# A hybrid encoder layer on one Trainium2 core: inverse rms multiplied onto the projection banks instead of onto x^T

## The chip, the cores and the metric

The kernel runs on one core of one Trainium2 chip. The core has five engines that run side by side, each with its own in-order queue of instructions: TensorE (matrix products, PE in the profile, with its weight loads as PEld), VectorE (DVE), ScalarE (ACT), GpSimd (POOL) and SyncE (SP, which here only issues DMAs). Products land in PSUM banks; everything else lies in SBUF or in device memory. The metric is device time in microseconds (us), the less the better.

## The reference

One layer over 1024 tokens of 1024 features. What matters here is its first part:

```python
def rmsnorm(x, g):
    y = xf * lax.rsqrt(jnp.mean(xf * xf, axis=-1, keepdims=True) + EPS) * g
...
    h = rmsnorm(x, g_mix_pre[l])
    proj = h @ w_in[l]
    # proj: fq, fk, fv (8 heads of 64), 8 gate columns, cq, ck, cv (8 heads of 64)
    y_fox = forgetting_attention(fq, fk, fv, f_logit)   # causal, with summed log-sigmoid gates
    y_chk = chunked_relpos_attention(cq, ck, cv, rel_bias[l])
    y = concat(rmsnorm(y_fox), rmsnorm(y_chk))
    x = x + rmsnorm(y @ w_out[l], g_mix_post[l])
    # then cross-attention into 256 memory tokens, and a squared-ReLU MLP, each with its norms
```

The inverse rms is one number for each token. The product with `w_in` sums over features, so the number can be multiplied onto a token's row of x before the product or onto its row of the product afterwards.

## The kernel before

All products are float32 made from two float32r parts: each operand is split into a high part (a rounded copy, ScalarE) and a low part (the rest, VectorE or GpSimd), and `mm3` (L174 to L176) issues three matmuls, high by high and the two mixed ones. x^T comes in two halves of 512 tokens (`th` = 0 and 1), each in 8 chunks `kc` of 128 features.

**The opening** (L1315 to L1521, an order written out by hand) loads x^T (`xf`), splits it with the gain alone (`plain_split`, L1384 and L1385) into `hT`, and computes the value banks of the first four head pairs and the gate columns in four rounds (`value_part`). In these banks tokens lie on the partitions, so the inverse rms (`rall`, from `square` and `root`) enters as one number per partition when they are emptied (`values_out`, L1438 to L1441). For queries and keys, and for the values of the later four pairs, tokens lie along the free axis. For them `spread` makes `rt[th]`, the inverse rms of 512 tokens along the free axis in all partitions; `norm` (L1413) multiplies it and the gain onto `xf`, and `norm_split` (L1418, L1419) splits the result into the same `hT` tiles again. `stock.split_now(2)` splits the first query and key weights (L311, L320), `gparts` are eleven steps of the gates (L381 to L394, log-sigmoid by exponential and logarithm, ending in `fe`), and `bias_rows` (L223 to L228) makes the relative-position rows that the chunked heads read later.

**The attention phase** is ordered by a planner, `Flow`. It keeps a clock in us (`flow.now`, 0 at its start), a cost for each step, due times for VectorE, ScalarE, GpSimd and the DMA queue (`flow.put`), and counted buffers (`Tokens`). It takes steps from several streams, the first that is ready in a fixed order: products of probabilities and values, turns (transposes of probabilities, L572 to L581), scores (L499 to L515), `side_steps`, and last `filler_steps`, which holds the projections (`project_steps`), the memory keys, the output projection and the memory values. The instructions are issued in the order that the planner finds, so each engine's queue is in that order. `flow.free` says from when an engine is free at the start.

`project_steps` computes a 128x512 bank for one pair of heads and one `th`: 24 matmuls into one of two `mm` banks. For queries and keys each half of the bank's partitions (one head) is then split: high part by ScalarE (L713, L720), low part by VectorE (L714, L721), both read from PSUM, and the bank is free when both low parts are done. Keys are copied to the other partitions by DMA. A value bank is copied by ScalarE (L693). Queries of pair 0 for `th` 0, its keys, then both for `th` 1 come first. `side_steps` starts with the transposes of the gates (`ftr`, L401) as soon as the flow clock is past 13, then copies, a running sum (`gate_scan`, L408), a store (`gate_store`), and the bias loads of the first heads wait for that store.

`u4` is a pool of 4 KB tiles (32 of them), of which `hT` holds 16 and the early values 8; the other 8 are counted tokens.

The opening's values in short: rounds (0,0), (1,0), (0,1), (1,1) of group and half; `rt0` is spread in the second round, `rt1` at the end of the third. Second phase and MLP follow with the same split products; no line of them is touched.

## Time and profile before

| what | us |
|---|---|
| median of 3 runs | 1488.63 |
| the runs | 1482.97, 1490.52, 1488.63 |
| the profiled execution | 1487.82 |
| its span, first to last instruction | 1486.0 |
| VectorE busy in the span | 921.0 |
| ScalarE busy | 804.0 |
| GpSimd busy | 387.4 |
| mean granted TensorE clock | 0.995 of full |

The profile is of one execution. Its page gives the busy time of each engine; further views give the busy time in chosen stretches, each engine's instructions in order of time, groups of equal instructions with the idle time ahead of them and what ended it, and who waited for whom. In a row such as `L714 DVE ... qs<-q,qs 64x512 fp32r<-64x512 f32 x32`, L714 is the line of the kernel, `qs<-q,qs` says what is written from what, and x32 how often. A part in square brackets such as `[7.03 <-DVE qs L714]` gives the idle time ahead of the instruction and what ended it.

### The profile page before, as it was taken

The page shows a single profiled execution, that of the slowest core. Times are in us where ns is not written, and L with a number is a line of the kernel's source. Part 1 is how long each engine was busy: PE and PEld are TensorE (multiplying, and loading weights), DVE is VectorE, ACT ScalarE, POOL GpSimd, SP SyncE. Part 2 cuts the span into 40 slices and gives each one's busy share as a digit, 9 for nine tenths or more (in the row PEclk, how much of TensorE's full clock was granted, in tenths as well). Part 3 has the DMA queues.
Part 4 walks back from the last instruction along what each step waited for, and adds up shares of the span by engine and source line. Part 5 has one row for each costly group of instructions (what it writes and reads, how often), then busy time and mean ns, then how long its engine had stood idle before and what let it go on. Part 6 is the DMA issues. An engine that isn't in the chain of part 4 may idle for free. (4 is left out here: it accounts for less than half of the span.)

```text
span 1486.0 us, 20873 instructions
## 1 busy us (share of the span) xinstructions
PE 1457.7 (98%) x7260; PEld 1228.0 (83%) x7260; DVE 921.0 (62%) x1590; ACT 804.0 (54%) x1426; POOL 387.4 (26%) x488
## 2 busy tenths in 40 slices
PE   8899999999999999999999999999999999999998
PEld 8778888888888887888888887888888888888886
DVE  4857676466466635874374687675555665656577
ACT  6637776576576753554353454555555553443442
POOL 1324565444343210431031413432223000000021
PEclk9999999999999999999999999999999999999999
DMA  8124555645437668461241446764445685445575
GB/s 327 29 87 118 127 111 106 194 135 117 116 90 186 174 189 326 143 212 58 85 170 57 138 160 230 241 237 155 150 156 170 244 344 183 142 136 205 176 249 198
DMA packets 101753, 247.90 MB, mean 167 GB/s; under 512 B 12152, under 2 KB 24576, under 8 KB 101648
## 3 DMA queue, kind: packets, MB, share of 16 engines
q1 hardware_dynamic: 97040, 238.18, 48.0%
q0 software_dynamic: 4608, 8.39, 4.1%
q8 instruction: 57, 0.93, 0.3%
q14 instruction: 48, 0.39, 0.1%
HBM read 174.64 MB, written 71.88 MB: 166 GB/s over the span
## 5 line engine op out<-in xcount | busy, mean ns | idle before, releaser
L578 DVE TENSOR_TENSOR p<-ptr,p 128x512 fp32r<-128x512 f32 (+1 forms) x152 | 92.3, 617 | 54.3 <-ACT p L581 53.6
L1916 ACT ACTIVATE whif<-ra 128x1024 fp32r<-128x1024 f32 x37 | 39.2, 1060 | 122.7 <-PE fy L175 62.6
L1918 DVE TENSOR_TENSOR wlof<-ra,whif 128x1024 fp32r<-128x1024 f32 x37 | 45.3, 1225 | 91.6 <-ACT whif L1916 91.5
L581 ACT ACTIVATE p<-ptr 128x512 fp32r<-128x512 f32 (+1 forms) x152 | 78.9, 539 | 39.9 <-PE ptr L572 39.0
L2032 POOL TENSOR_SCALAR rf<-sf 128x1 f32<-128x1 f32 x8 | 8.2, 1030 | 326.6 <-ACT jf L2017 326.3
L622 PE MATMUL pv<-p,vs 128*128 128x512 f32 (+1 forms) x304 | 85.9, 370 | 1.9 <-DVE p L578 1.9
L176 PE MATMUL fx<-vhif,wlof 128*128 128x512 f32 x168 | 65.4, 389 | 0.0
L174 PE MATMUL fx<-vhif,whif 128*128 128x512 f32 x168 | 65.4, 389 | 0.0
L175 PE MATMUL fx<-vlof,whif 128*128 128x512 f32 x168 | 65.4, 389 | 0.0
L622 PEld LDWEIGHTS pv<-p,vs 128*128 128x128 f32 x304 | 55.0, 189 | 12.5 <-DVE p L578 2.3
L1806 POOL TENSOR_TENSOR sc<-wf,wf 128x512 f32<-128x512 f32 x14 | 22.0, 1574 | 143.1 <-DMA wf<-in_w_ff 129.2
L174 PE MATMUL q<-hT_hi,whiq 128*128 128x512 f32 x128 | 52.2, 407 | 7.0 <-DVE qs L714 7.0
L174 PE MATMUL k<-hT_hi,whik 128*128 128x512 f32 x128 | 52.5, 410 | 0.0
L174 PE MATMUL mq<-h2T_hi,whimq 128*128 128x512 f32 x128 | 51.6, 403 | 0.0
L631 ACT ACTIVATE ot<-pv 128x512 f32<-128x512 f32 x64 | 38.0, 593 | 24.8 <-PE pv L622 23.2
L174 PE MATMUL yw<-whiwo,yT_hi 128*128 128x512 f32 x128 | 51.1, 399 | 0.0
L176 PE MATMUL q<-hT_hi,wloq 128*128 128x512 f32 x128 | 50.9, 398 | 0.1
L175 PE MATMUL q<-hT_lo,whiq 128*128 128x512 f32 x128 | 50.9, 397 | 0.0
L174 PE MATMUL ym<-whimo,oT_hi 128*128 128x512 f32 x128 | 50.3, 394 | 0.1
L176 PE MATMUL yw<-whiwo,yT_lo 128*128 128x512 f32 x128 | 50.4, 394 | 0.0
L175 PE MATMUL yw<-wlowo,yT_hi 128*128 128x512 f32 x128 | 50.3, 393 | 0.0
L175 PE MATMUL k<-hT_lo,whik 128*128 128x512 f32 x128 | 50.2, 392 | 0.0
(593 smaller groups left out, 4916.8 us busy)
## 6 DMA issues: line engine op xcount, KB each, us to landing
ra<-gd SPq DMA_DIRECT2D x56, 512.0 KB, 3.7
wg<-in_w_ff SPq DMA_DIRECT2D x56, 512.0 KB, 4.7
wf<-in_w_ff SPq DMA_DIRECT2D x38, 512.0 KB, 3.7
gd<-s SPq DMA_DIRECT2D x48, 256.0 KB, 2.1
od<-ot SPq DMA_DIRECT2D x64, 128.0 KB, 2.4
od<-od POOLq DMA_DIRECT2D x32, 256.0 KB, 4.5
wrawmq<-in_w_mq SPq DMA_DIRECT2D x16, 512.0 KB, 3.6
wrawmo<-in_w_mo SPq DMA_DIRECT2D x16, 512.0 KB, 3.9
```

The source lines that it names most:

```text
L174: nc.tensor.matmul(ps, lh, rh, start=start, stop=False, skip_group_check=more)
L175: nc.tensor.matmul(ps, lh, rl, start=False, stop=False, skip_group_check=more)
L176: nc.tensor.matmul(ps, ll, rh, start=False, stop=stop, skip_group_check=more)
L578: flow.put("V", at, 0.56 if dead else 0.7, lambda: nc.vector.tensor_sub(pl[:, live, :], tr[:, live, :], f(ph[:, live, :])), done)
L581: flow.put("S", flow.end, 0.49 if dead else 0.6, lambda ph=ph, tr=tr, live=live: nc.scalar.activation(ph[:, live, :], tr[:, live, :], AF.C ...
L622: nc.tensor.matmul(pv[:, :, q0 * P:(q0 + k1 - k0) * P], v, x[:, :, k0:k1, :].rearrange("p m k q -> p m (k q)"), start=c == 0 and m == 0, s ...
L631: nc.scalar.activation(box["t"][:, :, :, ::step], pv.rearrange("p m (k q) -> p m k q", q=P), AF.Copy)
L1806: eng.tensor_sub(sc[:, k1], r0[:, k0], r1[:, k0])
L1916: nc.scalar.activation(ah, ra, AF.Copy)
L1918: nc.vector.tensor_sub(al, ra, f(ah))
L2032: nc.gpsimd.tensor_scalar(r, ssf[b][:, 0:1], ssf[b][:, 1:2], EPS, op0=ALU.add, op1=ALU.add)
```

## The change

The second scaling and split of x^T in the opening goes. `hT` keeps the split of x^T with the gain alone. Each query, key or later value bank is multiplied by `rt[th]` as it is emptied: by one VectorE operation into a new float32 tile (`qn`, two buffers) for queries and keys, which are then split from that tile, or straight into `vt` for values. `rt` gets a tag of its own with two buffers. The counted `u4` tokens go from 8 to 7, the `u4` pool from 32 to 31 tiles, and the descriptor scratch of GpSimd's DMAs from 4096 to 1024 bytes per partition. In the opening the first two weight splits move ahead of the third round's `values_out`, the gate steps are no longer interleaved with norms, and squares 6 and 7 move ahead of the second round's `values_out`. The bias rows and their store become planned steps due at flow time 8, the gate transposes may start at flow time 5 instead of 13, and VectorE counts as free from 3.0 instead of 5.0.

```diff
-        return up.tile(list(shape), dt, tag="u4", bufs=32, name=name)
+        return up.tile(list(shape), dt, tag="u4", bufs=31, name=name)
...
-            dict(... ot=3, u4=8,
+            dict(... ot=3, qn=2, u4=7,
...
                 yield (0.681, lambda: kc or there((what, n)) and free["mm"].ready() and
-                       (th or free["u4"].ready(u) and (what != "k" or free["klo"].ready(2))))
+                       (what == "v" or free["qn"].ready()) and (th or free["u4"].ready(u) and (what != "k" or free["klo"].ready(2))))
...
-                flow.put("S", flow.end, 0.6, lambda th=th, ps=ps, cs=cs: nc.scalar.activation(vt[n][:, cs], ps, AF.Copy),
+                flow.put("V", flow.end, 0.7, lambda th=th, ps=ps, cs=cs: nc.vector.tensor_tensor(vt[n][:, cs], ps, rt[th], op=ALU.mult),
...
+            def scaled(ps=ps, box=box, th=th, nm=f"{what}n{n}_{th}"):
+                box["x"] = p1.tile([P, HT], F32, tag="qn", bufs=2, name=nm)
+                nc.vector.tensor_tensor(box["x"], ps, rt[th], op=ALU.mult)
+
+            def halves(at, box=box, th=th, cs=cs):
+                free["mm"].give(at)
+                left = all_of(("qn", what, n, th), 2, free["qn"].give)
+                for a, (own, oth) in enumerate(HALVES):
...
+                            nc.scalar.activation(kd[n, a][own, cs], box["x"][own], AF.Copy)
...
+                            nc.vector.tensor_sub(kl[n, a][own, cs], box["x"][own], f(kd[n, a][own, cs]))
...
+            flow.put("V", flow.end, 0.7, scaled, halves, 1)
...
-        yield 0.87, lambda: flow.now > 13.0 and free["tr"].ready(2)
+        yield 0.87, lambda: flow.now > 5.0 and free["tr"].ready(2)
...
-            r = p1.tile([P, HT], F32, tag="ot", bufs=3, name=f"rt{th}")
+            r = p1.tile([P, HT], F32, tag="rt", bufs=2, name=f"rt{th}")
...
-        def norm(th, kc):
-            x = xf[th][kc // 2][:, kc % 2, :]
-            nc.vector.scalar_tensor_tensor(x, x, gp[:, kc:kc + 1], rt[th], op0=ALU.mult, op1=ALU.mult)
-
-        def norm_split(th, kc):
-            x = xf[th][kc // 2][:, kc % 2, :]
-            h, l = hT[th].hi(kc), hT[th].lo(kc)
-            nc.scalar.activation(h, x, AF.Copy)
-            nc.vector.tensor_sub(l, x, f(h))
...
         gparts, gate_turn, gate_scan, gate_store = forget_gates()
+        stock.split_now(2)
         values_out(0, 1, V)
-        for call in gparts[:4]:
+        for call in gparts:
             call()
-        stock.split_now(2)
...
         values_out(1, 1, W)
         bias_rows(0)
-        bias_rows(1)
-        flow.put("D", 14.0, 0.55, lambda: nc.sync.dma_start(rd, rows[0]))
-        flow.free.update(V=5.0, S=3.0)
+        flow.put("V", 8.0, 2.0, lambda: bias_rows(1), lambda at: flow.load(at, lambda: nc.sync.dma_start(rd, rows[0])), 3)
+        flow.free.update(V=3.0, S=3.0)
...
-    nc = bacc.Bacc("TRN2", target_bir_lowering=False, num_devices=1, dynamic_dma_scratch_size=4096)
+    nc = bacc.Bacc("TRN2", target_bir_lowering=False, num_devices=1, dynamic_dma_scratch_size=1024)
```

More of the change, by code (lines that the diff above doesn't have):

```diff
@@ new lines, in project_steps, with hi, lo, then @@
+            free["qn"].take()
+            box = {}
+            def scaled(ps=ps, box=box, th=th, nm=f"{what}n{n}_{th}"):
[5 more added lines that the diff above has]
+                for a, (own, oth) in enumerate(HALVES):
+                    def hi(a=a, own=own):
+                        if what == "q":
+                            pv = box["x"].rearrange("p (a b) -> p a b", b=P)[:, :, ::1 if kind == "f" else -1]
+                            dst = qs[n, a].rearrange("p (a b) -> p a b", b=P)[:, th * 4:th * 4 + 4, :]
+                            nc.scalar.activation(dst[own], pv[own], AF.Copy, scale=-0.125)
+                        else:
+                            nc.scalar.activation(kd[n, a][own, cs], box["x"][own], AF.Copy)
+                    def lo(a=a, own=own, oth=oth):
+                        if what == "q":
+                            pv = box["x"].rearrange("p (a b) -> p a b", b=P)[:, :, ::1 if kind == "f" else -1]
+                            dst = qs[n, a].rearrange("p (a b) -> p a b", b=P)[:, th * 4:th * 4 + 4, :]
+                            nc.vector.scalar_tensor_tensor(dst[oth], pv[own], -0.125, f(dst[own]), op0=ALU.mult, op1=ALU.subtract)
+                        else:
+                            nc.vector.tensor_sub(kl[n, a][own, cs], box["x"][own], f(kd[n, a][own, cs]))
+                    copy = lambda x, own=own, oth=oth: nc.sync.dma_start(f(x[oth, cs]), f(x[own, cs]))
+                    def then(at, a=a, lo=lo, copy=copy):
+                        if what == "k":
+                            flow.load(at, lambda: copy(kd[n, a]), part, 2.3)
+                        flow.put("V", at, 0.63, lo, lambda end: (left(end), part(end) if what == "q" else flow.load(
+                            end, lambda: copy(kl[n, a]), part, 2.3)), 1)
+                    flow.put("S", at, 0.6, hi, then, 1)
@@ L1490, in build @@
         spread(1, d, "pv")
-        for kc in range(6, KC):
-            norm(0, kc)
-        for kc in range(KC):
-            norm_split(0, kc)
         W = value_banks(1, 1)
```

50 lines of the change are left out of this document (2 added, 48 removed).

## The prediction

> **What bounds the kernel now.** First the page: busy time by engine, and the 40 slices of 37.15 us.
>
> ```profile
> span 1486.0 us, 20873 instructions
> PE 1457.7 (98%) x7260; PEld 1228.0 (83%) x7260; DVE 921.0 (62%) x1590; ACT 804.0 (54%) x1426; POOL 387.4 (26%) x488
> PE   8899999999999999999999999999999999999998
> ```
>
> TensorE is busy for all but 28.3 us of the span, and only the first, second and last slices show gaps. The change removes no matmul, so it can pay only where TensorE stands still or runs slowly. The busy time in stretches of 10 us around the opening's end, and three later ones of 100 us, show where (columns after the length: busy us and instructions of PE, PEld, DVE, ACT, POOL, then the granted clock, DMA share, GB/s):
>
> ```profile
> 60.00:70.00 10.00, 9.23 (x41) 7.32 (x39) 9.07 (x14) 6.29 (x12) 3.54 (x3) 1.00 0.37 105
> 70.00:80.00 10.00, 3.74 (x9) 2.97 (x10) 7.44 (x14) 5.00 (x9) 5.18 (x4) 0.73 0.31 96
> 80.00:90.00 10.00, 10.00 (x47) 7.87 (x45) 3.65 (x3) 2.30 (x4) 0.00 (x0) 0.93 0.46 136
> 200.00:300.00 100.00, 99.15 (x533) 83.70 (x532) 60.61 (x168) 66.74 (x139) 50.13 (x82) 1.00 0.58 143
> 300.00:400.00 100.00, 100.00 (x552) 85.59 (x551) 62.77 (x187) 68.87 (x148) 41.05 (x57) 1.00 0.46 117
> 400.00:500.00 100.00, 98.06 (x620) 87.91 (x619) 62.34 (x181) 68.69 (x142) 41.59 (x53) 1.00 0.55 139
> ```
>
> From 70 to 80 us TensorE does 3.74 us of work at a granted clock of 0.73 while VectorE is full before it (9.07 of 10 us). From 200 to 500 us TensorE loses 2.8 us in all. The list of waits names the releaser of the gap; beside it the longest later wait on VectorE:
>
> ```profile
> PE q L174 <- DVE qs L714: 7.0, 1, 7.0
> PE pv L622 <- DVE p L578: 1.9, 1, 1.9
> ```
>
> The timeline of each engine says what was late (start, duration, engine, line, what). TensorE:
>
> ```profile
> 63.40 0.39 PE L176 MATMUL q<-hT_hi,wloq 128*128 128x512 f32 x1
> 63.63 0.39 PE L174 MATMUL k<-hT_hi,whik 128*128 128x512 f32 x1
> 68.84 0.39 PE L176 MATMUL k<-hT_hi,wlok 128*128 128x512 f32 x1
> 76.26 0.77 PE L174 MATMUL q<-hT_hi,whiq 128*128 128x512 f32 x1 [7.03 <-DVE qs L714]
> 80.24 1.58 PE L401 MATMUL ftr<-ident,fe 128*8 128x128 f32 x8
> 81.58 0.48 PE L174 MATMUL q<-hT_hi,whiq 128*128 128x512 f32 x1
> ```
>
> ScalarE and VectorE over the same time:
>
> ```profile
> 65.16 4.26 ACT L1418 ACTIVATE hT_hi<-xf 128x512 fp32r<-128x512 f32 x8
> ...
> 70.75 1.06 ACT L311 ACTIVATE whiq<-wrawq 128x1024 fp32r<-128x1024 f32 x1
> 72.65 1.19 ACT L713 ACTIVATE qs<-q 64x512 fp32r<-64x512 f32 x2
> 67.53 0.23 DVE L394 SCALAR_TENSOR_TENSOR fe<-fz,fe 128x64 f32<-128x64 f32 x1
> 67.67 3.70 DVE L1419 TENSOR_TENSOR hT_lo<-xf,hT_hi 128x512 fp32r<-128x512 f32 x6
> 71.28 1.66 DVE L1441 SCALAR_TENSOR_TENSOR vs<-v,rall,vs 128x256 fp32r<-128x256 f32 x4
> 73.34 1.37 DVE L228 COPY rrow<-rrow 8x511 f32<-8x511 f32 x1
> 74.73 1.39 DVE L714 SCALAR_TENSOR_TENSOR qs<-q,qs 64x512 fp32r<-64x512 f32 x2
> ```
>
> The first query bank is complete at 63.8 us (63.40 + 0.39), the first key bank at 69.2. Both `mm` banks are then full, and the next query product needs one back. Emptying the query bank is queued behind the second split of the right half of x^T (L1418, L1419), the value banks and the bias rows: ScalarE reaches it at 72.65, VectorE at 74.73, and TensorE resumes at 76.26. By then its second-half operands are also only just there (the last L1419 ends at 71.4).
>
> **The change part by part.** *The stall.* The key product's 24 matmuls start every 0.2265 us ((68.84 − 63.63)/23), so without a wait the next one would start at 69.07. It and what follows up to 81.58 are nine q matmuls and eight gate transposes: 12.51 us. At full pace the nine take 2.04. The eight transposes take 1.34 slow (81.58 − 80.24); matmul pace there is 0.44 ((80.24 − 76.26)/9), about half speed, so I take 0.67. Sum 2.71, **gain 9.8 us**: 7.2 of standing and 2.6 of slow clock. Without the second part being true it is 7.2.
>
> [...] The trace shows 5.3 us of slow work here, so the rows decide.
>
> *What has to be early for this.* Removed from the opening (groups between 36 and 77 us):
>
> ```profile
> L1413 DVE SCALAR_TENSOR_TENSOR xf<-xf,gp,rt 128x512 f32<-128x512 f32 x16 | 14.2, 938 | 0.0
> L1419 DVE TENSOR_TENSOR hT_lo<-xf,hT_hi 128x512 fp32r<-128x512 f32 x16 | 9.9, 687 | 3.4 <-ACT hT_hi L1418 3.4
> L1418 ACT ACTIVATE hT_hi<-xf 128x512 fp32r<-128x512 f32 x16 | 8.5, 617 | 0.0
> ```
>
> That is 24.1 us of VectorE and 8.5 of ScalarE, all ahead of the first bank. Two rows of ScalarE, the spread of `rt1` and its last gate column, place what is left:
>
> ```profile
> 46.47 0.60 ACT L1408 ACTIVATE rt<-rt 128x512 f32<-128x512 f32 x1 [5.67 <-PE rt L1406]
> 53.01 0.31 ACT L1440 ACTIVATE fcol<-v,rall 128x8 f32<-128x8 f32 x1
> ```
>
> ScalarE goes from `rt1` (over at 47.1) straight to the two first weight splits (2 x 1.06), the value banks and the gates. The last value banks are full when the first query product starts (63.40 − 23 x 0.2265 = 58.2) and take about 2 us (four times 0.4 on each engine, L1441 for one of them), so VectorE is free by 60.5. The scaling of the first query bank starts when that bank is full, near 63.8, and frees it after one VectorE instruction, near 64.6: 4.5 us before TensorE asks. The bias rows (1.4 us and a little) now follow behind it; even ahead of it with the gates' scan they would free the bank by 69. Their store and reload serve only the chunked heads, which come after all four pairs of the others.
>
> *The gate transposes* move from flow time 13 to 5, about 63 us. They stand in TensorE's in-order queue, and everything behind them waits if `fe` is late. Its chain waited in before for ScalarE and for VectorE's norms; alone it is the eight sums of `fz`, two table loads like the one below, and ten small operations like L394 (0.23):
>
> ```profile
> 54.01 0.70 DVE L381 TENSOR_TENSOR fz<-fcol,bfgt 128x8 f32<-128x8 f32 x8
> 63.70 1.28 ACT L391 ACT_TABLE_LOAD   x1 [4.74 <-DVE fe L390]
> 82.48 2.28 DVE L408 TENSOR_TENSOR_SCAN fla<-fea 8x1024 f32<-8x1024 f32 x1 [4.92 <-ACT fea L405]
> ```
>
> That is 0.7 + 2.6 + 2.3, some 5.6 us, from the last gate column, which ScalarE writes near 51.4 (47.1 + 2.1 + the 2.2 that the column took behind the last split) instead of 53.3: ready at 57 to 58.5, 5 us ahead. Cost 0. Their scan (2.3 us on VectorE) ends near 68, so the store of its row and the first bias loads, which now stand ahead of the key copies on SP, hold back no copy: the first key half is split near 71.
>
> *Added work.* Forty bank scalings (16 query, 16 key, 8 value banks), each a 128x512 VectorE operation with one PSUM and one SBUF input; that is the form of L578. Eight ScalarE copies of value banks go. The split halves then read SBUF, not PSUM:
>
> ```profile
> L578 DVE TENSOR_TENSOR p<-ptr,p 128x512 fp32r<-128x512 f32 x72 | 49.3, 688 | 23.2 <-ACT p L581 22.8
> L693 ACT ACTIVATE vt<-v x8: 578/598/606, 267.2 to 441.4; 128x512 f32<-128x512 f32 x8
> L721 DVE TENSOR_TENSOR kl<-k,kd x32: 664/690/696, 76.1 to 461.9; 64x512 fp32r<-64x512 f32 x32
> L1413 DVE SCALAR_TENSOR_TENSOR xf<-xf,gp,rt x16: 739/747/1792, 36.2 to 64.2; 128x512 f32<-128x512 f32 x16
> L320 POOL TENSOR_TENSOR wloq<-wrawq,whiq x16: 1274/1295/1927, 56.5 to 392.4; 128x512 fp32r<-128x512 f32 x16
> ```
>
> 40 x 0.688 = 27.5 us on VectorE, spread over some 410 us: its share there rises from 62% to 68 or 69%. ScalarE loses 4.8 us; its split halves go from 0.59 to about 0.62 (L1418, from SBUF), 64 x 0.025 = 1.6 back. Neither is the bound.
>
> The 64 low halves become operations with two SBUF inputs. With a PSUM input those of the keys never varied (0.664 to 0.696); L1413, with two SBUF inputs, went from 0.747 to 1.792 beside GpSimd's weight split, which itself went from 1.295 to 1.927. So a collision costs up to 1.05 us of VectorE and 0.63 of GpSimd. GpSimd is busy 41 to 50%; with that share colliding, for half the price each, VectorE pays 64 x 0.45 x 0.52 = 15 us, another 3.6%.
>
> [...]
>
> What lands on TensorE I bound by −1 us (a bank held for 0.7 instead of some 2.6 us; of the 2.8 us lost between 200 and 500 us no listed wait is for such a bank) and by +34 us (one full collision price for half of the 64). TensorE's waits on VectorE with VectorE at 62% are the 1.9 above and some smaller; at 72% they may grow by half. I take **+1.0**.
>
> *The rest at 0.* `u4` with 31 buffers: no wait named here is for one; if the memory keys start late for it, scores and turns run meanwhile, and without these TensorE would stand for as long as the delay. The smaller descriptor scratch touches the accumulating DMAs of GpSimd:
>
> ```profile
> od<-od POOLq DMA_DIRECT2D x32, 256.0 KB, 4.5
> ```
>
> There are 32 in some 380 us, so hardly ever more than a few in flight; if each had to wait for the last to land, GpSimd would lose 4.5 us a time, 144 in all, and the turns with it. The two weight splits, moved ahead, find GpSimd idle and free their raw buffers, so the next weight load on SP only gets earlier. The key copies come 0.7 us later for their bank; the next pair's products cover that, as they cover the whole way to the first scores now, and uncovered it would delay the first scores by 0.7.
>
> Sum: 1487.82 − 9.8 + 1.0 = **1479.0** for the profiled execution; the runs' median stands 0.8 above it (1488.63), so 1479.8.
>
> **The rivals.** *Most of it is given back in attention*: VectorE at 72% with collisions makes score and turn waits of 3 to 9 us. For: ScalarE and VectorE already pass work to each other in 23.2 us of idle ahead of L578; against: 38% of VectorE is free. Time 1483 to 1487, say 1485.
>
> *The gates come late.* `fe` was ready at 67.76 in before; if it were that late again, TensorE would stand from 63.2 for 4.5 us and then run slowly for as much as 2.6: gain 9.8 − 7.1, about 1486. Against: the chain's 5.6 us.
>
> *Slower: collisions in the low halves.* It decides from nine or ten of the 64 that each put a full 1.05 us on TensorE's path; with 20 it is 21 us: 1488.6 − 9.8 + 21 = 1500; with half of them, 1513. For: GpSimd also normalises the probabilities that the turns wait for. Against: query and key evacuations lie 5.4 us apart, and no score waits on the pair at hand.
>
> **How the numbers follow.** Forecast 0.66 (1476 to 1481.5); given back 0.18; gates late 0.06; slower 0.10. About 0.5%, 7.4 us, is what a measurement can tell here (the three runs spread over 7.5 us), so faster means below 1481.2. The forecast nearly all (0.62) and a little of the case given back (0.03): 0.65; within: 0.25; slower 0.10. The range: the full 9.8, the −1 and 3 us of scatter give 1474.5; upwards it takes in the cases up to 1487.
>
> **What would show it.** Right: no wait of TensorE between 58 and 90 us; granted clock 1.00 from 70 to 90; the gate transposes near 63 us, unslowed; the scaling right behind each bank; about 27 us more VectorE between 70 and 480 us, with some low halves above 1 us; first scores some 10 us earlier. Wrong: a gap at 63 us ahead of the transposes, a new wait on `qn` or on VectorE among the scores and turns, or an attention stage that ends less than 8 us earlier than before.

## The result and the profile after

The changed kernel takes 1475.31 us (median of 5 runs, 1474.34 to 1475.99) beside 1484.23 us of the kernel before in the same comparison (5 runs, 1482.53 to 1490.52): ratio 0.9929, 95% interval 0.9904 to 0.9955. Run twice more beside other kernels it gave 0.9914 (0.9899 to 0.9929) and 0.9921 (0.9902 to 0.9940). The middle one of the three is 0.79% faster, some 11.7 us of 1486; the forecast was 8.8 us. The profiled executions differ by 12.5 us (1486.0 and 1473.5). The median of three runs from which the prediction started, 1488.63, lay at the high end: in five later comparisons, 17 runs each, the kernel before has medians of 1485.08 to 1487.80.

The page of the changed kernel: span, busy time, slices.

```profile
span 1473.5 us, 20806 instructions
PE 1453.8 (99%) x7260; PEld 1225.4 (83%) x7260; DVE 931.9 (63%) x1598; ACT 793.7 (54%) x1402; POOL 398.2 (27%) x488
PE   8999999999999999999999999999999999999998
```

The gap of the second slice is gone. Idle TensorE time fell from 28.3 to 19.7 us, and its busy time from 1457.7 to 1453.8 with the same 7260 matmuls: some of them had run slowly. The same stretches as in the prediction (length; busy us and instructions of PE, PEld, DVE, ACT, POOL; granted clock, DMA share, GB/s):

```profile
60.00:70.00 10.00, 10.00 (x49) 8.13 (x49) 5.34 (x9) 3.81 (x6) 5.04 (x4) 1.00 0.33 107
70.00:80.00 10.00, 10.00 (x46) 8.26 (x45) 4.34 (x7) 2.52 (x4) 0.00 (x0) 1.00 0.31 72
80.00:90.00 10.00, 10.00 (x46) 8.28 (x45) 4.33 (x8) 2.52 (x4) 0.89 (x2) 1.00 0.51 143
200.00:300.00 100.00, 99.41 (x530) 83.51 (x528) 69.06 (x179) 65.94 (x137) 52.06 (x76) 1.00 0.56 138
300.00:400.00 100.00, 100.00 (x542) 85.57 (x542) 68.57 (x177) 63.08 (x132) 41.98 (x55) 1.00 0.48 120
400.00:500.00 100.00, 98.94 (x635) 88.94 (x634) 71.35 (x199) 71.46 (x149) 40.33 (x51) 1.00 0.58 155
```

From 70 to 80 us TensorE is full at a clock of 1.00 (before: 3.74 us at 0.73). VectorE's share from 200 to 500 us went from 62% to 70%, and TensorE lost 1.65 us there instead of 2.79.

VectorE's timeline of the changed kernel around the first query bank (start, duration, engine, line, what; in brackets the idle time before it and its releaser); below it the row of the gate transposes, with the shortest, median and longest ns and the first and last start:

```profile
58.68 0.23 DVE L394 SCALAR_TENSOR_TENSOR fe<-fz,fe 128x64 f32<-128x64 f32 x1
58.83 1.65 DVE L1442 SCALAR_TENSOR_TENSOR vs<-v,rall,vs 128x256 fp32r<-128x256 f32 x4
64.10 0.69 DVE L708 TENSOR_TENSOR qn<-q,rt 128x512 f32<-128x512 f32 x1 [3.62 <-PE q L176]
67.22 2.28 DVE L408 TENSOR_TENSOR_SCAN fla<-fea 8x1024 f32<-8x1024 f32 x1 [0.25 <-ACT fea L405]
...
70.45 0.69 DVE L708 TENSOR_TENSOR kn<-k,rt 128x512 f32<-128x512 f32 x1 [0.23 <-PE k L176]
```

```profile
L401 PE MATMUL ftr<-ident,fe x8: 270/272/273, 63.9 to 64.7; 128*8 128x128 f32 x8
```

VectorE is done with the value banks at 60.5 and waits 3.6 us for TensorE; the bank is scaled 0.2 us after it is full and free at 64.8. `fe` is ready at 58.9, 5.0 us ahead of the transposes, which run at 0.27 us each.

The groups of VectorE from 60 to 500 us (busy, mean ns of one | idle before them); the first two of before, the others of the changed kernel:

```profile
L714 DVE SCALAR_TENSOR_TENSOR qs<-q,qs 64x512 fp32r<-64x512 f32 x32 | 22.0, 689 | 23.3 <-ACT qs L713 18.6 <-PE q L176 4.1
L721 DVE TENSOR_TENSOR kl<-k,kd 64x512 fp32r<-64x512 f32 x32 | 22.0, 688 | 25.1 <-ACT kd L720 24.6
```

```profile
L726 DVE SCALAR_TENSOR_TENSOR qs<-qn,qs 64x512 fp32r<-64x512 f32 x32 | 27.3, 853 | 5.8 <-ACT qs L718 4.9
L728 DVE TENSOR_TENSOR kl<-kn,kd 64x512 fp32r<-64x512 f32 x32 | 27.3, 852 | 9.4 <-ACT kd L720 8.9
L708 DVE TENSOR_TENSOR kn<-k,rt 128x512 f32<-128x512 f32 x16 | 11.0, 688 | 11.3 <-PE k L176 11.3
L708 DVE TENSOR_TENSOR qn<-q,rt 128x512 f32<-128x512 f32 x16 | 11.0, 686 | 12.1 <-PE q L176 12.0
L693 DVE TENSOR_TENSOR vt<-v,rt 128x512 f32<-128x512 f32 x8 | 5.5, 682 | 1.4 <-PE v L176 1.4
```

The forty scalings take 27.5 us. The 64 low halves, now with two SBUF inputs, went from 44.0 to 54.6 us.

Three rows divide the span: the first query product, the first score and the first product of the memory queries (first and last start behind the durations). Before, then after:

```profile
L174 PE MATMUL q<-hT_hi,whiq x128: 387/389/767, 57.8 to 416.6; 128*128 128x512 f32 x128
L499 PE MATMUL sf0g<-kd,qs x12: 277/389/497, 97.3 to 112.2; 128*128 128x512 f32 x5, 128*128 128x256 f32 x4, 128*128 128x384 f32 x3
L174 PE MATMUL mq<-h2T_hi,whimq x128: 389/389/486, 627.5 to 811.7; 128*128 128x512 f32 x128
```

```profile
L174 PE MATMUL q<-hT_hi,whiq x128: 387/389/486, 58.4 to 406.7; 128*128 128x512 f32 x128
L499 PE MATMUL sf0g<-kd,qs x12: 277/363/475, 87.9 to 103.7; 128*128 128x512 f32 x5, 128*128 128x256 f32 x4, 128*128 128x384 f32 x3
L174 PE MATMUL mq<-h2T_hi,whimq x128: 389/389/486, 614.9 to 799.1; 128*128 128x512 f32 x128
```

First query product to first score, A: 39.5 to 29.5 us. First score to first memory query, B: 530.2 to 527.0. From there to the end: 858.5 and 858.6. The first query product itself starts anywhere between 55.8 and 59.1 us whatever the kernel, so A and B tell apart what spans blur. They come from the one profiled execution of each kernel, as differences of starts given to 0.1 us, and the ratio comes from all its runs. The profiled executions of remove_only and values_on_act were the slowest of theirs (1479.46 beside a median of 1475.13, 1485.89 beside 1481.75), so their B is on the high side. All profiled kernels:

```
kernel             ratio  (95% interval)       A      B      A+B
before             -                           39.5   530.2  569.7
before_again       0.9998 (0.9985 to 1.0012)   39.7   526.9  566.6
scratch_only       1.0003 (0.9992 to 1.0015)   39.3   529.4  568.7
u4_only            1.0041 (1.0026 to 1.0057)   43.6   529.7  573.3
buffers_only       1.0047 (1.0033 to 1.0060)   40.9   532.5  573.4
bias_late          0.9988 (0.9975 to 1.0000)   37.7   527.9  565.6
short_gap          0.9952 (0.9933 to 0.9970)   34.5   529.3  563.8
remove_only        0.9927 (0.9913 to 0.9941)   29.5   531.9  561.4
remove_again       0.9932 (0.9913 to 0.9951)   29.5   530.1  559.6
values_only        0.9937 (0.9917 to 0.9956)   29.5   525.5  555.0
after              0.9929 (0.9904 to 0.9955)   29.5   527.0  556.5
after_again        0.9914 (0.9899 to 0.9929)   29.5   525.9  555.4
after_third        0.9921 (0.9902 to 0.9940)   29.4   526.1  555.5
placement_back     0.9914 (0.9898 to 0.9930)   29.5   526.1  555.6
scale_twice        0.9918 (0.9899 to 0.9937)   30.1   527.4  557.5
low_from_bank      0.9928 (0.9915 to 0.9942)   31.2   527.1  558.3
values_on_act      0.9974 (0.9962 to 0.9987)   29.5   537.2  566.7
order_kept         0.9930 (0.9912 to 0.9948)   29.5   526.3  555.8
order_moved        0.9987 (0.9977 to 0.9998)   29.5   536.1  565.6
```

### The profile page after: what moved, and what is told of

It is laid out like the page before. It is cut to its first block, busy times and chain, and to the rows that moved or that the text cites. A ratio compares the mean times of both kernels' runs of the same rounds, so it can differ in the third digit from the quotient of the medians.

```text
span 1473.5 us, 20806 instructions
## 1 busy us (share of the span) xinstructions
PE 1453.8 (99%) x7260; PEld 1225.4 (83%) x7260; DVE 931.9 (63%) x1598; ACT 793.7 (54%) x1402; POOL 398.2 (27%) x488
## 5 line engine op out<-in xcount | busy, mean ns | idle before, releaser
L176 PE MATMUL k<-hT_hi,wlok 128*128 128x512 f32 x128 | 50.2, 392 | 0.0
L175 PE MATMUL mq<-h2T_lo,whimq 128*128 128x512 f32 x128 | 50.0, 391 | 0.0
```

What stands on the lines that cost most here:

```text
L175: nc.tensor.matmul(ps, lh, rl, start=False, stop=False, skip_group_check=more)
L176: nc.tensor.matmul(ps, ll, rh, start=False, stop=stop, skip_group_check=more)
```

## The experiments

### The parts of the change in the opening

**before_again**: the kernel before, unchanged.

> The kernel before, unchanged, for a second profile. Theory A (the time beyond the forecast comes from a stall late in attention that hangs on one DMA and on the clock): the wait of 7.0 us near 69 us is there again to within 0.2 us, and the stall near 512 us (1.9 us, then a granted clock below 1 for some 4 us) differs from the first profile by a microsecond or more, so the span differs by 1 to 4 us. Rival B (the change's edits in attention gave it): the second profile repeats the first, stall near 512 us included, and the span is 1486 within 1 us.

The wait of 7.0 us repeats, and A is 39.7. The wait of 1.9 us at `pv`, the longest of attention in the first profile, shrinks to 0.2, and the slow matmuls behind it are gone too; B is 3.3 us shorter. Theory A holds: the profile from which the prediction started had this much more in attention than the next one of the same kernel.

**remove_only**: the normalisation of x^T alone is taken out, with nothing in its place, so queries, keys and the later values leave out the inverse rms.

```diff
-        for kc in range(2):
-            norm(0, kc)
...
-        for kc in range(2, KC):
-            norm_split(1, kc)
```

> The kernel before without the second scaling and split of x^T, and without anything in its place: queries, keys and the later values leave out the inverse rms. All other edits of the change are absent. Theory A (the gain is the opening's stall alone, the added bank scalings cost TensorE nothing): the wait near 69 us is gone, the first score starts 9 to 10 us earlier than in the kernel before, and the time equals the changed kernel's to within 2 us (1473 to 1477). Rival B (the added scalings or collisions cost TensorE something that the gain hides): it is 3 us or more faster than the changed kernel. Rival C (the change's other edits, placement or buffers, give part of the gain): it is 3 us or more slower than the changed kernel.

A = 29.5, the same as with the whole change: the removal alone earns the opening's 10 us. The time, 1475.13 us beside 1485.59, is that of theory A.

**placement_back**: the changed kernel with the gates, the bias rows and VectorE's booked start as before.

```diff
-        yield 0.87, lambda: flow.now > 5.0 and free["tr"].ready(2)
+        yield 0.87, lambda: flow.now > 13.0 and free["tr"].ready(2)
...
-        flow.put("V", 8.0, 2.0, lambda: bias_rows(1), lambda at: flow.load(at, lambda: nc.sync.dma_start(rd, rows[0])), 3)
-        flow.free.update(V=3.0, S=3.0)
+        bias_rows(1)
+        flow.put("D", 14.0, 0.55, lambda: nc.sync.dma_start(rd, rows[0]))
+        flow.free.update(V=5.0, S=3.0)
```

> The changed kernel with three placements of the kernel before: gate transposes from flow time 13, bias rows ahead of the planned steps with their store at 14, VectorE free from 5.0. Theory A (the removed work alone clears the way for the first bank): no wait near 69 us, time within 1.5 us of the changed kernel, first score up to 4 us later but TensorE filled with the next projections. Rival C (the placement does part of it): a wait of 1 us or more comes back between 64 and 80 us, 2 us or more slower than the changed kernel.

0.9914 and A = 29.5: these three moves neither cost nor earn anything that can be told.

### Which queue was late

**bias_late**: the kernel before, with the second bias rows behind the bank instead of ahead of it.

```diff
-        bias_rows(1)
-        flow.put("D", 14.0, 0.55, lambda: nc.sync.dma_start(rd, rows[0]))
+        flow.put("V", 19.0, 2.0, lambda: bias_rows(1), lambda at: flow.load(at, lambda: nc.sync.dma_start(rd, rows[0])), 3)
```

> The kernel before with the bias rows planned at flow time 19 instead of ahead of the first low halves, nothing else. Theory A (the first bank is held by what stands ahead of it on VectorE): the wait of 7.0 us shrinks by the rows' 1.9 us to 5.1, the nine query products behind it still run at half speed for about 4 us, time 2 us less than the kernel before. Rival H (ScalarE's order, not VectorE's, holds the bank): the wait shrinks by less than 1 us.

The wait only falls from 7.0 to 6.15 us, which is the sign of rival H and not the 5.1 of theory A. Timeline of TensorE, ScalarE and VectorE in this kernel:

```profile
76.71 0.76 PE L174 MATMUL q<-hT_hi,whiq 128*128 128x512 f32 x1 [6.15 <-DVE qs L714]
73.95 1.19 ACT L713 ACTIVATE qs<-q 64x512 fp32r<-64x512 f32 x2
75.17 1.39 DVE L714 SCALAR_TENSOR_TENSOR qs<-q,qs 64x512 fp32r<-64x512 f32 x2 [0.94 <-ACT qs L713]
```

VectorE is now early and waits 0.94 us for ScalarE, which runs its own queue without a pause (splits, value banks, two weight splits) until 73.95. The two queues were nearly equally late: taking the rows' 1.9 us (72.85 to 74.71 in the kernel before) out of one gains 0.9 and moves the bound to the other.

**short_gap**: the same, and without six of the eight splits of the second half.

```diff
-        for kc in range(2, KC):
-            norm_split(1, kc)
```

> As bias_late, and six of the eight second splits of the right half of x^T left out (chunks 2 to 7 of it keep the split with the gain alone, so queries and keys of the right half mix scaled and unscaled chunks). Theory A: VectorE and ScalarE reach the first bank some 3.5 us earlier still, the wait is 1.5 to 3 us. If the slow pace needs a gap longer than that, the products behind it run at full pace and the time is 8 to 9 us below the kernel before; if any gap of some us brings it, 5.5 to 7 us below.

TensorE's timeline:

```profile
73.19 0.77 PE L174 MATMUL q<-hT_hi,whiq 128*128 128x512 f32 x1 [3.05 <-DVE qs L714]
73.76 0.63 PE L175 MATMUL q<-hT_lo,whiq 128*128 128x512 f32 x1
...
75.46 0.63 PE L176 MATMUL q<-hT_hi,wloq 128*128 128x512 f32 x1
...
76.18 0.40 PE L175 MATMUL q<-hT_lo,whiq 128*128 128x512 f32 x1
```

A gap of 3.05 us is followed by six matmuls some 0.43 us apart instead of 0.2265; the seventh (75.89) is on pace again, 2.7 us after the first. A falls by 5.0 us (39.5 to 34.5), 3.95 by the shorter gap and about 1 by the shorter slow stretch. The gap of 3.05 us lies at the end of the expected 1.5 to 3, and the pace behind it is slow all the same. The time falls by 0.48%, some 7 us, the upper end of the case with the slow pace.

### The buffers

**buffers_only, u4_only, scratch_only**: the kernel before with 31 `u4` buffers (tokens 7) and the smaller descriptor scratch, and with each alone.

```diff
-        return up.tile(list(shape), dt, tag="u4", bufs=32, name=name)
+        return up.tile(list(shape), dt, tag="u4", bufs=31, name=name)
...
-            dict(s=2, tr=2, pv=2, mm=2, sp=5, p=2, klo=4, bias=2, raw=2, w=2, ot=3, u4=8,
+            dict(s=2, tr=2, pv=2, mm=2, sp=5, p=2, klo=4, bias=2, raw=2, w=2, ot=3, u4=7,
...
-    nc = bacc.Bacc("TRN2", target_bir_lowering=False, num_devices=1, dynamic_dma_scratch_size=4096)
+    nc = bacc.Bacc("TRN2", target_bir_lowering=False, num_devices=1, dynamic_dma_scratch_size=1024)
```

> The kernel before with 31 u4 tiles, 7 counted tokens and the descriptor scratch of 1024 bytes, nothing else. Theory A: no change that can be told, within 3 us of the kernel before; the accumulating DMAs of GpSimd issue in 0.84 us and land in 4.5 us as before. Rival C (buffers reorder the end of attention for the better): 3 us or more faster. Rival D (they cost something): slower by 2 us or more, with waits of GpSimd between the accumulating DMAs above 24.6 us in all.

> The kernel before with 31 u4 tiles and 7 counted tokens, scratch as it was. Theory F (the 7 us of the three buffer edits together come from the planner, which finds another order with one token less): 1.003 to 1.006 of the kernel before, first memory key product some 5 us later after the first score than in the kernel before. Rival G (they come from the descriptor scratch): within 0.1% of the kernel before.

> The kernel before with 1024 bytes of descriptor scratch instead of 4096 and nothing else. Theory F: within 0.1% of the kernel before, accumulating DMAs issue in 0.84 and land in 4.5 us. Rival G: 1.003 to 1.006, with longer issues or landings of these DMAs.

The scratch costs nothing (1.0003). One `u4` buffer less costs the kernel before 0.41%, some 6 us, and with the scratch 0.47%. Theory F of u4_only has the size right and the place wrong: the first memory key product comes 1.9 us later after the first score, not 5, and A grows by 4.1. In buffers_only GpSimd's waits between its accumulating DMAs stay at 23.9 us, so the time of theory D came without its sign. ScalarE and TensorE in `u4_only`:

```profile
85.31 0.59 ACT L720 ACTIVATE kd<-k 64x512 fp32r<-64x512 f32 x1 [10.87 <-PE q L175]
87.49 0.47 PE L174 MATMUL k<-hT_hi,whik 128*128 128x512 f32 x1 [2.05 <-DVE kl L721]
```

ScalarE needs the second `kd` tile and waits 10.87 us for the last query product: the four weight tiles of the first query and key live in `u4` and no token counts them. With 16 tiles of x^T, 8 of the value banks, these 4, two `qs` and two `kd`, 32 are wanted. Behind the late split the key bank stays full, and TensorE waits. The changed kernel has the same wait, 3.92 us long:

```profile
75.72 0.63 ACT L720 ACTIVATE kd<-kn 64x512 fp32r<-64x512 f32 x1 [3.92 <-PE q L175]
```

There the bank went free with the scaling, 4.6 us earlier (L708 on `kn`: 70.45 + 0.69), and TensorE does not wait. low_from_bank, next, takes this early return away, and a wait of TensorE comes back.

**low_from_bank**: the changed kernel, with the low halves read from the bank, which is given back after both; the low halves then leave out the inverse rms.

```diff
-                free["mm"].give(at)
-                left = all_of(("qn", what, n, th), 2, free["qn"].give)
...
+                held = all_of(("mmq", what, n, th), 2, free["mm"].give)
+                back = all_of(("qn", what, n, th), 2, free["qn"].give)
+                left = lambda end: (held(end), back(end))
...
-                            nc.vector.tensor_sub(kl[n, a][own, cs], box["x"][own], f(kd[n, a][own, cs]))
+                            nc.vector.tensor_sub(kl[n, a][own, cs], ps[own], f(kd[n, a][own, cs]))
```

> The changed kernel, but the low halves of queries and keys read the bank in PSUM and not the scaled tile, so a bank is held until both low halves are done, and the low halves have one SBUF input each; what they compute leaves out the inverse rms, the high halves keep it. Theory A (the collisions cost VectorE some 10 us and TensorE nothing): the low halves go back to 0.69 us each, the sum of VectorE between 60 and 500 us falls by about 10 us, the time stays within 2 us of the changed kernel. Rival B (collisions cost TensorE something): 2 us or more faster. Rival E (a bank that is free after one operation is what makes the changed kernel proof against fewer buffers, which cost the kernel before 7 us): 3 us or more slower, with a wait of a projection on a low half.

The groups of VectorE, and TensorE's timeline after the gap:

```profile
L727 DVE SCALAR_TENSOR_TENSOR qs<-q,qs 64x512 fp32r<-64x512 f32 x32 | 22.0, 688 | 5.9 <-ACT qs L719 5.0
L729 DVE TENSOR_TENSOR kl<-k,kd 64x512 fp32r<-64x512 f32 x32 | 22.0, 687 | 9.6 <-ACT kd L721 9.1
```

```profile
75.15 0.50 PE L174 MATMUL k<-hT_hi,whik 128*128 128x512 f32 x1 [1.28 <-DVE kl L729]
75.48 0.39 PE L175 MATMUL k<-hT_lo,whik 128*128 128x512 f32 x1
```

The low halves are back at 44.0 us, so their 10.6 us are the price of the second SBUF input. Two rows of the changed kernel show how it falls (shortest, median and longest ns):

```profile
L726 DVE SCALAR_TENSOR_TENSOR qs<-qn,qs x32: 684/687/2981, 65.5 to 422.6; 64x512 fp32r<-64x512 f32 x32
L728 DVE TENSOR_TENSOR kl<-kn,kd x32: 665/690/1673, 71.8 to 452.8; 64x512 fp32r<-64x512 f32 x32
```

The median is as before. The 24 of the 64 that no GpSimd instruction overlaps take at most 0.69 us; of the 40 others, twelve take more than 1 us, the longest 2.98. Yet without the collisions nothing gets faster: 1474.89 us beside 1472.57 of the changed kernel on the same chip, intervals overlapping. This run does not show that they cost TensorE nothing, because it adds waits of its own: A is 1.7 us longer by the wait that the early return had hidden, and attention has a wait of 2.64 us at a score (459.30, `sc6g`) that the changed kernel lacks. Without the latter B would be some 2 us shorter than the changed kernel's mean of 526.3 (527.1 − 2.64 = 524.5), so up to about 2 us of collisions on TensorE's path stay possible, by one profile.

### The load on VectorE

**scale_twice**: the changed kernel, every scaling issued twice, those of the value banks too, and the planner told 1.4 us for both.

```diff
-                nc.vector.tensor_tensor(box["x"], ps, rt[th], op=ALU.mult)
+                for _ in range(2):
+                    nc.vector.tensor_tensor(box["x"], ps, rt[th], op=ALU.mult)
...
-            flow.put("V", flow.end, 0.7, scaled, halves, 1)
+            flow.put("V", flow.end, 1.4, scaled, halves, 1)
```

> The changed kernel with each of the 40 bank scalings issued twice, the planner told 1.4 us for both: 27.5 us more on VectorE, which is then at about 78% between 100 and 480 us. Theory A (VectorE has slack enough, the scalings cost TensorE nothing): within 3 us of the changed kernel. Rival B (VectorE is near the point where it decides): 6 us or more slower, with waits of TensorE on L578 or the scores' reductions above 5 us in all.

The scalings take 55.0 us instead of 27.5 and the ratio is 0.9918, beside 0.9921 of the changed kernel (**after_third**) on the same chip. In its profile A is 0.7 us and B 1.1 us longer than in the changed kernel, and the time can't be told apart. VectorE has that much room; most of attention's length does not hang on it.

> The changed kernel, unchanged, beside the others on one chip. Theory A: 0.9915 to 0.9940 of the kernel before, its span within 2 us of the first profile; TensorE's waits between the first score and the memory queries again 2 to 4 us in all.

> The changed kernel, unchanged, for a third profile and for times beside the others. Theory A: 10.0 us from the first query product to the first score less than in the kernel before (29.5 against 39.5), and 0.991 to 0.994 of its time.

Both repeat the first comparison: 0.9914 and 0.9921, A = 29.5 and 29.4, and in after_again 3.12 us of waits of TensorE between the first score and the memory queries. The span of after_again is 2.8 us shorter than that of the first profile (1470.7 beside 1473.5), somewhat more than the 2 us allowed.

### Why attention became shorter

B was 528.8 us in the mean over the first three kernels of the table and is 526.3 in the three profiles of the changed kernel. Five kernels ask where this comes from.

**remove_again, values_only, values_on_act**: the first has neither scalings nor the value move, the second moves the value copies alone to VectorE, the third is the changed kernel with them back on ScalarE. All three leave out the inverse rms of the later values, the first two that of queries and keys as well. The edit of the second, beside that of remove_only:

```diff
-                flow.put("S", flow.end, 0.6, lambda th=th, ps=ps, cs=cs: nc.scalar.activation(vt[n][:, cs], ps, AF.Copy),
+                flow.put("V", flow.end, 0.7, lambda th=th, ps=ps, cs=cs: nc.vector.tensor_copy(vt[n][:, cs], ps),
```

> The kernel before without its normalisation of x^T, a second time (this leaves out the factor 1/rms of query, key and value). The length of the stretch from the first score to the first product of the memory queries is what is asked for: 526.9 to 530.2 us in three profiles with the order of the kernel before, 531.9 in the first of this kernel, 525.9 to 527.0 in three of the changed kernel. If the 2.5 us are scatter of one run to the next: between 526 and 530 here. If the new emptying of the banks earns them: 529 or more again, and a time of 0.992 to 0.994 of the kernel before.

> The same kernel, with the eight value banks copied by VectorE and not by ScalarE (the factor 1/rms is still left out); query and key banks are emptied as in the kernel before. If relieving ScalarE's queue of these copies is what shortens attention: a stretch of 526 to 527.5 us, and a time of 0.991 to 0.992. If the early return of query and key banks does it: 529 to 532 us and the ratio of the kernel with the normalisation removed, 0.9927. If it is scatter: no order between this one and that.

> The changed kernel, with the eight value banks copied by ScalarE as before (this leaves out the factor 1/rms of the values); query and key banks are scaled by VectorE as in the change. If the early return of query and key banks shortens attention: 526 to 527.5 us, 0.991 to 0.992. If the value copies do it: 529 to 532 us, 0.9927 to 0.994. If it is scatter: anything from 526 to 532, and a time that can't be told from the changed kernel's 0.992.

With the copies on VectorE B is 525.5, with them on ScalarE 530.1 and 531.9 (nothing else changed) or 537.2 (in the changed kernel, more than any of its three cases allowed). In time the first pair can't be told apart (0.9937 and 0.9932; values_only lacks the 0.991 to 0.992 of its first case), the second clearly: 0.9974 against 0.9914 to 0.9929. The 8 copies are only 4.8 us of ScalarE, so either that load or the order that the planner writes out must be what counts.

**order_kept, order_moved**: the changed kernel, with the engine and the booking taken apart. The first copies on ScalarE but is booked on VectorE; the second scales on VectorE, as in the change, but is booked on ScalarE.

```diff
 order_kept
-                flow.put("V", flow.end, 0.7, lambda th=th, ps=ps, cs=cs: nc.vector.tensor_tensor(vt[n][:, cs], ps, rt[th], op=ALU.mult),
+                flow.put("V", flow.end, 0.7, lambda th=th, ps=ps, cs=cs: nc.scalar.activation(vt[n][:, cs], ps, AF.Copy),
 order_moved
-                flow.put("V", flow.end, 0.7, lambda th=th, ps=ps, cs=cs: nc.vector.tensor_tensor(vt[n][:, cs], ps, rt[th], op=ALU.mult),
+                flow.put("S", flow.end, 0.6, lambda th=th, ps=ps, cs=cs: nc.vector.tensor_tensor(vt[n][:, cs], ps, rt[th], op=ALU.mult),
```

> The changed kernel; the eight value banks are copied by ScalarE (this leaves out the factor 1/rms of the values), but the planner books the copy on VectorE as in the change, so the order of all other work stays that of the changed kernel. With planner and copy both on ScalarE the ratio was 0.9974, the stretch from the first query product to the first product of the memory queries 566.7 us, against 555.4 to 556.5 in three profiles of the changed kernel. If the order that the planner writes out makes the difference: 0.991 to 0.993 and 555 to 558 us. If ScalarE's load by eight copies does it (4.8 us of it): 0.996 to 0.998 and 563 us or more.

> The changed kernel whole, with the planner booking the scaling of the eight value banks on ScalarE though VectorE does it. If the order that the planner writes out makes the difference: 0.996 to 0.998, 563 us or more from the first query product to the first memory query. If ScalarE's load does it: 0.991 to 0.993 and 555 to 558 us.

This separates them: order_kept 0.9930 and B = 526.3, order_moved 0.9987 and B = 536.1, on the same chip. Together with the changed kernel (both on VectorE, 0.9914 to 0.9929) and values_on_act (both on ScalarE, 0.9974) all four pairs of engine and booking are measured: booking decides, not the engine. What the other order does is seen at the hand-over from attention to the output. SyncE's issues in order_moved, then in the changed kernel (start, time of the issues, x count):

```profile
547.74 2.71 SPq L1053 DMA_DIRECT2D yw<-yd  x4
550.50 0.43 SPq L214 DMA_DIRECT2D g_mix_post<-in_g_mix_post  x1
552.16 0.33 SPq L214 DMA_DIRECT2D g_mem_pre<-in_g_mem_pre  x1
552.53 1.20 SPq L1004 DMA_DIRECT2D xtw<-in_x  x2
554.74 1.62 SPq L298 DMA_DIRECT2D wrawmv<-in_w_mv  x2
```

```profile
544.38 2.46 SPq L1053 DMA_DIRECT2D yw<-yd  x4
546.94 0.42 SPq L298 DMA_DIRECT2D wrawmv<-in_w_mv  x1
548.09 0.33 SPq L214 DMA_DIRECT2D g_mix_post<-in_g_mix_post  x1
```

The changed kernel issues one of the last two loads of the memory value weights ahead of the gains and of `xtw`; in order_moved both stand behind them. ScalarE and TensorE of order_moved show what follows; then the window of 560 to 580 us of order_moved, and TensorE's wait and the same window of the changed kernel:

```profile
565.09 1.06 ACT L311 ACTIVATE whimv<-wrawmv 128x1024 fp32r<-128x1024 f32 x1 [6.50 <-DMA wrawmv<-in_w_mv]
566.20 0.80 PE L174 MATMUL mv<-whimv,mT_hi 128*128 128x512 f32 x1 [2.81 <-ACT whimv L311]
```

```profile
560.00:580.00 20.00, 15.85 (x55) 11.82 (x55) 7.80 (x8) 7.09 (x8) 0.00 (x0) 0.83 0.70 240
```

```profile
563.69 0.50 PE L174 MATMUL mv<-whimv,mT_hi 128*128 128x512 f32 x1 [0.49 <-ACT whimv L311]
```

```profile
560.00:580.00 20.00, 18.75 (x81) 14.69 (x80) 11.70 (x14) 8.32 (x13) 0.00 (x0) 1.00 0.82 283
```

TensorE stands for 2.81 us and then runs at half pace (0.43 us a matmul until 572.7). In the changed kernel the same product waits 0.49 us and the clock of that window is 1.00. This place holds 5.7 of the 9.1 us by which B of order_moved exceeds the changed kernel's first profile (first `mv` at 546.8, mq at 623.6: 76.8; changed: 543.8 and 614.9: 71.1); the other 3.4 lie ahead of it, a wait of 2.05 us for a memory key weight among them.

## Why the prediction was right and wrong

Part by part, in the two profiled executions on which the sum was built: A fell by 10.0 us (forecast 9.8), B fell by 3.2 (forecast: 1.0 longer), the first query product came 0.6 later and the rest took 0.1 more. Together that is 12.5 us less where 8.8 were forecast. The measured 1475.31 us lies below the 1476 to 1481.5 that the prediction gave its forecast. The step that failed is the term for attention, and a starting time that was too high hid behind it.

**Right: the opening.** A fell by 10.0, 10.2 and 9.9 us in three pairs of profiles (before and after, before_again and after_again, scratch_only and after_third); the forecast was 9.8. Of before's 28.3 us of idle TensorE, 7.0 stood here, and the slow stretch behind it is gone. That this gap was paid twice, by standing and by the slow stretch, is borne out from the other side by short_gap (A 5.0 us shorter: 3.95 and about 1). That the slow part came out so close is partly luck: it repeated in the three profiles above, but behind an equal gap of 7.03 us in buffers_only the slow matmuls lasted 2.7 us instead of 5.3, which would make the gain some 1.3 us less.

**Right: what had to be early.** `fe` was ready at 58.9 (57 to 58.5 forecast), the transposes ran at 63.9 at full speed, and the scaling stood right behind its bank, so "the gates come late" fell. VectorE was named as the late queue with ScalarE 2 us ahead of it; bias_late shows that ScalarE was nearly as much the bound. The change empties both, so the sum did not suffer.

**Right in mechanism, off in size: collisions.** 10.6 us of VectorE against 15. That is 0.17 us a piece in the mean (10.6 / 64), against the 0.23 assumed (0.45 x 0.52). Some low halves above 1 us were named as a sign, and twelve are. In before, with one PSUM input, 34 of the 64 overlap a GpSimd instruction and none takes more than 0.70 us; in the changed kernel, with two SBUF inputs, 40 do, and the twelve are among them. VectorE's busy time between 70 and 480 us rose by 32.7 us (254.8 to 287.5) and not by the 27 named, which left the collisions out. The slower rival needed nine or ten collisions that reach TensorE in full; low_from_bank leaves room for about 2 us of them.

**Wrong: "I take +1.0" for attention.** The step was that TensorE's waits grow by half when VectorE is fuller, and that nothing works the other way. They shrank. From the first score to the first memory query TensorE stood for 6.05, 4.63 and 7.00 us in before, before_again and scratch_only, and for 4.11, 3.12 and 3.31 in the three profiles of the changed kernel. The means, 5.9 and 3.5, make 2.4 of the 2.5 us by which B shrank; TensorE's busy time there stayed at 523. Against the +1.0 this is 3.5 us, about the 3 us by which the gain was larger than forecast (11.7 against 8.8). The load itself may have been sized rightly: in scale_twice 27.5 us more of it go with 5.31 us of waiting and a B 1.1 us longer, by one profile, and the times can't tell it. Waits of 3 to 9 us, as "given back in attention" has them, are out by the same run.

What went is a wait for a weight of the memory keys (0.9, 0.7 and 1.8 us before) and two short ones of the value turns (0.5 and 0.3); waits of 0.5 and 0.2 at `pv` are new. The prediction left out that the planner writes the order of every queue from the engine and cost booked for each piece, so that a changed booking re-sorts loads that come some 100 us later as well. The memory key wait bears this out: it stands in all eleven profiled kernels that book the value banks on ScalarE, 0.2 to 2.8 us long, and in none of the eight that book them on VectorE, whichever engine works. In time the booking of these eight pieces is worth 0.57% between order_moved and order_kept, and 0.58 to 0.73% between order_moved and the changed kernel, which use the same engine; that is several times the term. But the bad order of order_moved is not the order of the kernel before, so this does not say how much of before's 2.5 us is booking and how much scatter (526.9 to 530.2): values_only has B at 525.5 and yet no shorter time than remove_again. That share stays open.

**Wrong: "`u4` with 31 buffers at 0".** The edit is not free: 6 us in the kernel before, with a wait of 10.87 us on ScalarE. The sum did not show it because the early return of the bank hides it in the changed kernel; low_from_bank, without that return, has A 1.7 us longer. The prediction asked only about memory keys and missed the four weight tiles that no token counts.

**The starting point.** The time predicted was 4.5 us above the measured one. By the first comparison alone (1484.23 − 1475.31 = 8.9 us) the gain equals the forecast and all of the 4.5 is the high median of the first three runs; by the middle of the three ratios some 3 of it are attention. The first interval allows both. A gain of 8.8 us would be a ratio of 0.9941, and the intervals of the two repeats end below it, at 0.9929 and 0.9940, which speaks for the second. The profile that the sum started from was itself a long one: its B holds 3.3 us that before_again lacks, mainly a wait of 1.9 us and the slow matmuls behind it. The lower end of the range, by its own terms, is 1474.8 and not 1474.5 (1488.6 − 9.8 − 1 − 3).

## What to carry to other kernels

Where a planner writes the order of the queues, the engine and cost booked for a step are themselves an edit: run the step with its old booking and its old engine separately before crediting either. Price a wait of TensorE as the gap plus the slow matmuls after it, and give the second part a range, since the same gap may bring them or not (behind 7.0 us they lasted 5.3 us in before and 2.7 in buffers_only; behind 1.86 and 1.85 us the clock was 0.72 in remove_only and 1.00 in remove_again). Take more than one profile of the kernel before: what one shows late in the program may not be in the next. Look for all queues that are equally late before crediting one of them. Count every tile that lives in a pool, not only those the planner counts; a buffer taken away can be hidden by another part of the same change.

## What the hardware showed

- After a gap of 2.81 us (order_moved) and of 3.05 us (short_gap) TensorE's matmuls started 0.43 us apart instead of 0.2265, for 2.7 us in short_gap and until 572.75, some 6 us, in order_moved, where a second gap of 0.46 us lay inside. After 1.28 us (low_from_bank) the next ones kept full pace, 0.23 us apart.
- The length of the gap alone does not decide. The same kernel had the same wait at `pv` in two profiles, 1.86 us in remove_only and 1.85 in remove_again; the 6 us behind it ran at a granted clock of 0.72 in the first and 1.00 in the second:

```profile
503.49:509.49 6.00, 6.00 (x22) 4.82 (x23) 3.23 (x5) 3.83 (x8) 1.32 (x2) 0.72 0.67 165
501.38:507.38 6.00, 6.00 (x29) 4.96 (x30) 3.23 (x5) 4.29 (x10) 0.84 (x1) 1.00 0.68 164
```

- A gap of 2.05 us ahead of the same key product was followed by half pace after the first matmuls in u4_only (a clock of 0.72 over the next 6 us) and by full pace in buffers_only (1.00); the longest gap in attention with a clock of 1.00 behind it is the 2.64 us of low_from_bank.
- The same 64x512 operation on VectorE took 0.69 us in the mean with one PSUM input (before, low_from_bank), and 0.85 with two SBUF inputs in the changed kernel, beside a GpSimd that was busy 40 to 52% of the time.
- The start of the first query product scatters from 55.8 to 59.1 us over kernels, two profiles of one kernel by up to 1.9 us (58.4 and 56.5 of the changed one), so the span alone could not have shown a difference of 3 us in attention.
